# A two-layer encoder trunk whose instructions are recorded first and issued in the order of a list schedule of its own

## The chip, the cores and the metric

One Trainium2 core runs the whole program; the other cores of the chip are idle. The metric is the device time of one execution in microseconds. Times of runs are medians over several executions; durations of single instructions come from one profiled execution. The engines are named as the profile names them: PE is the matmul engine and PEld its weight loads, DVE the vector engine, ACT the scalar engine, POOL the general engine, SP the engine that issues the DMAs. Each engine takes its instructions strictly in the order in which they stand in its own queue, and the queues wait for one another by semaphores.

## The reference

The input is x of 256 tokens by 1024 features in float32. Two layers follow, and a last RMSNorm. A layer, cut to what matters:

```python
h = rmsnorm(x, norm_g[l])
proj = h @ w_in[l]                                   # 1024 x 18688
y_a = hgrn2_mixer(...) * silu(a_g)                   # A: gated recurrence, 8 heads, two directions
y_b = retention_mixer(...) * silu(b_g)               # B: retention, 8 heads, two directions
y_c = rwkv7_mixer(...) * silu(c_g)                   # C: delta rule, 16 heads, two directions
gates = sigmoid(merge.reshape(b, t, 3, D_MODEL))
mixed = gates[0] * (y_a @ w_branch_a) + gates[1] * (y_b @ w_branch_b) + gates[2] * (y_c @ w_branch_c)
x = x + mixed @ w_out
```

## The kernel before, in words

**Weights.** A layer has 93 blocks of weights, 1024 rows by 256 columns, and each block comes in two halves of 128x1024 values (`load_w`, lines 177 to 192). A half is loaded by SP into `wr`; ACT rounds it to float32r into `wh` (line 184); DVE subtracts, `wl = wr - wh` (line 187). Each of the three has a ring of three buffers (`RW = (3, 3, 3)`). A product with h or with a mixer's output is three float32r matmuls per 128 rows (`feat_mm`, line 200, and `tok_mm`, line 210): high by high, high by low, low by high. So a half block feeds 24 matmuls of 256 columns, and the two layers have 2 x 93 x 48 = 8928 of them. All others are float32; in the trace such a matmul stands as two, a transpose as one.

**Mixers.** C works on pairs of heads, p = 0 to 7. `c_prep` (projections `p_rk` and `p_vg`, decays, the products `c_p` of lines 393 to 395 from operands that DVE writes, among them `bbd`, line 388), `c_solve` (the inverse of 32 x 32 blocks: a trip through DRAM into `c_M`, then a chain of small DVE steps that begins at line 425 and goes through `c_tq`, lines 439 to 444) and `c_scan` (the products `c_o`, `c_ox`, `c_oy`, and the state from chunk to chunk, `c_st`, whose copy `c_sb` ACT makes). C runs two pairs ahead (`LA = 2`). Between the pairs stand the parts of A (p = -1 to 2) and of B (p = 3 to 6). A head of A makes its scores in eight steps on one PSUM bank: matmuls into `a_p` (lines 622, 623, 638, 658), then a copy or masked copy by ACT or DVE into `a_pt` (lines 640, 642, 659), then the next step on the same bank. PSUM's eight banks are split as pj 2, c 2, n 2, s 1, ab 1 (`PB`).

**Tail.** `tail` makes the three gates (`p_mg`), the branch products (`t_o`) and `w_out` (`pj`), 28 blocks of a layer; then `norm_T` makes the next layer's h.

**What sets the order.** The code calls the engines directly, in the order of the program text. Tiles come from pools, and the framework's scheduler (`schedule_with_timeline_sim=True`) puts each engine's instructions into their final order when the program is built. A pool that closes between the mixers and the tail gives its memory to the tail's tiles.

Of the kernel before, what the change touches and what calls it, by code (L numbers as in the profile page):

```python
# [2 lines left out]

# [12 lines left out]
L = 2  # L16
D = 1024
# [10 lines left out]
RW = (3, 3, 3)  # L28
# [4 lines left out]
# columns of a layer's packed parameters  # L33
# [9 lines left out]
# columns of the shape constants  # L43
# [9 lines left out]
# of the masks that A takes, and of the rotation that B takes  # L53
# [4 lines left out]
# blocks of weights in a layer, in the order of _blocks()  # L58
# [3 lines left out]
def _blocks():  # L62
    """(key, matrix, row range start, list of (column start, width)) of each block of 1024 rows and 256 columns."""
# [29 lines left out]

@with_exitstack
def trunk(ctx: ExitStack, tc, x, wb, pp, lora, cst, gtab, ng, out, parts="ABCT", layers=L, dbg=None):
    nc = tc.nc
    V, S, G, PE = nc.vector, nc.scalar, nc.gpsimd, nc.tensor

    keep = ctx.enter_context(tc.tile_pool(name="keep", bufs=1))
    wp = ctx.enter_context(tc.tile_pool(name="wp", bufs=1))  # L100
    ps = ctx.enter_context(tc.tile_pool(name="ps", bufs=1, space=bass.MemoryType.PSUM))
    dr = ctx.enter_context(tc.tile_pool(name="dr", bufs=2, space=bass.MemoryType.DRAM))

    S.preload_act_table_set("natural_log_exp_and_others")
# [4 lines left out]
    first = ExitStack()  # L109
    npool = first.enter_context(tc.tile_pool(name="np", bufs=1, side="right"))  # L110
    xs = npool.tile([128, 2, D], F32, name="xs")
    gb = npool.tile([128, D], F32, name="n_g")
    nc.sync.dma_start(xs[:, 0], x_src[:, 0])
    nc.sync.dma_start(C[:, 0:NFST], cst[:, 0:NFST])
    nc.sync.dma_start(xs[:, 1], x_src[:, 1])
    nc.sync.dma_start(gb, ng[0:1].to_broadcast([128, D]))
# [8 lines left out]
    nc.sync.dma_start(C[:, NFST:], cst[:, NFST:NCST])  # L125
    P_ = []
    for l in range(L):
        t = keep.tile([128, NP], F32, name=f"pp{l}")
        nc.sync.dma_start(t, pp[l])
        P_.append(t)  # L130

    turn = {}

    def ring(pool, shape, dt, tag, n, name):
        """a tile in the next of a tag's n buffers, in turn"""
        i = turn[tag] = (turn.get(tag, -1) + 1) % n
        return pool.tile(shape, dt, tag=f"{tag}{i}", bufs=1, name=name)
# [5 lines left out]
    DP = []  # L143
    for l in range(L):
# [3 lines left out]
        # 1 - mu0 - mu1  # L148
# [7 lines left out]
    # lower bounds: softmax over the layers with its maximum, cumulated, less the first  # L156
# [13 lines left out]
    # cumsum - p[0]  # L170
# [6 lines left out]
    def load_w(l, key):  # L177
        """the parts of a block's halves"""
        W = []
        for h in range(2):  # L180
            raw = ring(wp, [128, 1024], F32, "wr", RW[0], "wr")
            nc.sync.dma_start(raw, wb[2 * (l * NBLK + BK[key]) + h])
            hi = ring(wp, [128, 1024], F32R, "wh", RW[1], "wh")
            S.copy(hi, raw)  # L184
            lo = ring(wp, [128, 1024], F32R, "wl", RW[2], "wl")
            n = WS[h]
            V.tensor_sub(lo[:, 0:n], raw[:, 0:n], hi[:, 0:n].bitcast(F32))  # L187
            if n < 1024:
                G.tensor_sub(lo[:, n:], raw[:, n:], hi[:, n:].bitcast(F32))
# [13 lines left out]
    def tok_mm(o, W, t, h):  # L203
        """o[t, column] = h[:, t-tile]^T W; a half of the block holds four k-tiles"""
# [25 lines left out]
    def silu_from(pool, src, shape, tag, tmp, bufs=1, tb=1):  # L230
        """silu of a projection in PSUM"""
# [8 lines left out]
    def norm_T(xs, ss, gb, pool):  # L240
        """xs and the sums of its squares by token; gb: the gains, on every partition"""
# [63 lines left out]
    def c_prep(l, p, codes, pool):  # L305
        """Everything of pair p up to the chunk products, evacuated and masked."""
# [44 lines left out]
        # its ninth block holds the stacked identity  # L351
# [4 lines left out]
        # bonus: sum of r k_d r_k over both directions  # L356
# [7 lines left out]
        # k~, beta~, alpha~, r~ of each direction, and the products within its chunks  # L364
# [6 lines left out]
        for d in range(2):  # L371
            # a chunk's blocks of 64: A_rk^T, r~, A_ak, A_rb^T, beta' (first alpha~), A_ab^T, k', diag g, alpha~^T
            z = pool.tile([128, 4, 9, 64], F32, tag="c_Z", bufs=ZB, name="c_Z")
# [17 lines left out]
            for c in range(4):  # L391
                o = ps.tile([128, 8, 64], F32, tag="c", bufs=PB["c"], name="c_p1")
# [10 lines left out]
    def c_solve(l, p, st, pool):  # L403
        """Inverses of the diagonal 32 x 32 blocks of I - A_ab, one block and every fourth column a partition."""
        Z = st["Z"]
        s1 = dr.tile([4, 8, 32, 32], F32, tag="s1", name="s1")
        for hb in range(4):
            b = hb % 2
            for d in range(2):
                nc.sync.dma_start(s1[hb, 4 * d:4 * d + 4].rearrange("u j i -> j u i"),  # L410
                                  Z[d][32 * hb:32 * hb + 32, :, 5, 32 * b:32 * b + 32])
# [533 lines left out]
```

## Time and profile before

| | us |
|---|---|
| median of 3 runs (1818.41 to 1823.13) | 1823.03 |
| the profiled execution: span from its first to its last instruction | 1821.9 |
| PE busy in it | 1667.6 |
| PEld busy | 1625.0 |
| DVE busy | 1415.4 |
| ACT busy | 1056.5 |
| POOL busy | 322.0 |

Of the profiled execution the trace has its span alone, 1821.9 us, which lies 1.1 us below the median of the runs, so one can be read for the other. In the trace an instruction stands with its start and its duration; a row's last columns tell how long its engine was idle before it and which instruction's end released it. Matmuls overlap: one lasts about 0.28 us from start to result, while the next can start 0.12 us after it, so a PE that is busy need not be a PE at its best rate. PEclk is the granted clock as a share of full speed.

### The profile page before, as it was taken

To read this page: it belongs to the slowest core of one execution; us is meant where nothing else is said; L and a number is where in the kernel's file an instruction comes from. 1 tells how busy PE (TensorE), PEld (TensorE's weight loads), DVE (VectorE), ACT (ScalarE), POOL (GpSimd) and SP (SyncE) were. 2 spreads that over 40 slices of the span, in tenths; PEclk is the share of its full clock that TensorE was granted. 3 is DMA by queue.
4 is the path that set the end of the run, shared out by engine and by line. 5 is a ranking of instruction groups with operands and counts; after the bars stand their busy time and mean duration, and the time that the engine had idled before them with its cause. 6 is when DMAs were issued, how large, how long until landed. Compare 5 with 4: busy or idle time off the path is not lost.

```text
span 1821.9 us, 33791 instructions
## 1 busy us (share of the span) xinstructions
PE 1667.6 (92%) x12960; PEld 1625.0 (89%) x12960; DVE 1415.4 (78%) x2597; ACT 1056.5 (58%) x1940; POOL 322.0 (18%) x312
## 2 busy tenths in 40 slices
PE   6888899999999999999888789988999999999997
PEld 6877899898999998999888788988889999999997
DVE  5799898998878785565657989989998787846554
ACT  5665566757465545555556556757573656456453
POOL 1122222212120200010011222223131202100100
PEclk9989999999999999999988889999999999999999
DMA  6333223324344443755533233233244444437653
GB/s 221 116 118 105 79 96 102 117 86 138 119 155 141 146 148 133 244 200 187 198 114 118 99 100 91 88 109 107 93 133 125 144 142 154 142 131 245 208 186 116
DMA packets 127873, 250.30 MB, mean 137 GB/s; under 512 B 62304, under 2 KB 66784, under 8 KB 127456
## 3 DMA queue, kind: packets, MB, share of 16 engines
q1 hardware_dynamic: 127712, 248.15, 41.6%
q8 instruction: 102, 1.67, 0.4%
q14 instruction: 59, 0.48, 0.1%
HBM read 229.22 MB, written 14.68 MB: 134 GB/s over the span
## 4 chain that ended last, share of the span: by engine, by line
PE 49%; DVE 30%; issue 7%; DMA 6%; ACT 4%; SPq 2%; POOL 0%; DVEq 0%; ACTq 0%; POOLq 0%
PE t_o L200 10%; PE p_mg L200 8%; DVE wl L187 7%; DVE c_tq L439 3%; PE p_bv L210 3%; PE p_vg L200 3%; PE p_bg L200 2%; DMA c_M<-s 2%; PE pj L210 2%; PE c_p L393 2%; DMA s<-c_Z 2%; ACT wh L184 2%; DVE c_ts L441 2%; PE p_rk L200 1%; PE c_p L395 1%
## 5 line engine op out<-in xcount | busy, mean ns | idle before, releaser
L187 DVE TENSOR_TENSOR wl<-wr,wh 128x1024 fp32r<-128x1024 f32 x372 | 475.9, 1280 | 192.3 <-ACT wh L184 190.9
L184 ACT CAST wh<-wr 128x1024 fp32r<-128x1024 f32 x372 | 388.4, 1045 | 272.7 <-PE t_o L200 56.2
L200 PE MATMUL t_o<-yh,wh 128*128 128x256 f32 x512 | 144.7, 284 | 2.8 <-ACT yh L748 2.8
L200 PE MATMUL t_o<-yl,wh 128*128 128x256 f32 x512 | 145.0, 284 | 0.5 <-DVE yl L749 0.5
L200 PE MATMUL t_o<-yh,wl 128*128 128x256 f32 x512 | 144.6, 283 | 0.0
L608 POOL TENSOR_TENSOR a_sl<-a_kq,a_e 128x256 f32<-128x256 f32 x80 | 80.9, 1015 | 230.9 <-ACT a_e L618 66.0
L200 PE MATMUL p_mg<-h_hi,wh 128*128 128x256 f32 x384 | 109.6, 285 | 0.0
L200 PE MATMUL p_mg<-h_hi,wl 128*128 128x256 f32 x384 | 109.4, 285 | 0.0
L200 PE MATMUL p_mg<-h_lo,wh 128*128 128x256 f32 x384 | 108.7, 283 | 0.0
L200 PEld LDWEIGHTS t_o<-yh,wh 128*128 128x128 f32 x512 | 97.6, 191 | 3.2 <-ACT yh L748 3.2
L200 PEld LDWEIGHTS t_o<-yl,wh 128*128 128x128 f32 x512 | 97.9, 191 | 1.0 <-DVE yl L749 0.9
L200 PEld LDWEIGHTS t_o<-yh,wl 128*128 128x128 f32 x512 | 97.9, 191 | 0.0
L393 PE MATMUL c_p<-c_Z,bbd 128*128 128x192 f32 x256 | 68.9, 357 | 29.7 <-DVE bbd L388 25.0
L439 DVE TENSOR_TENSOR c_tq<-W,c_M 128x16 f32<-128x16 f32 (+6 forms) x112 | 89.0, 795 | 1.4
L200 PE MATMUL p_vg<-h_hi,wh 128*128 128x256 f32 x256 | 78.1, 305 | 8.1 <-ACT c_k L288 4.1
L399 ACT COPY c_Z<-c_p 128x192 f32<-128x192 f32 x128 | 40.3, 318 | 74.9 <-DVE c_Z L396 73.7
L200 PE MATMUL p_bg<-h_hi,wl 128*128 128x256 f32 x256 | 75.0, 293 | 4.6 <-DVE wl L187 4.6
L210 PE MATMUL p_bv<-wh,h_hi 128*128 128x256 f32 x256 | 76.1, 297 | 1.1 <-ACT b_z L694 1.1
L210 PE MATMUL p_bv<-wl,h_hi 128*128 128x256 f32 x256 | 75.4, 295 | 1.7 <-DVE wl L187 1.7
L200 PE MATMUL p_vg<-h_lo,wh 128*128 128x256 f32 x256 | 75.8, 296 | 0.0
L200 PE MATMUL p_vg<-h_hi,wl 128*128 128x256 f32 x256 | 75.6, 295 | 0.0
L210 PE MATMUL p_bv<-wh,h_lo 128*128 128x256 f32 x256 | 74.7, 292 | 0.0
(334 smaller groups left out, 5983.3 us busy)
## 6 DMA issues: line engine op xcount, KB each, us to landing
wr<-in_wb_dram SPq DMA_DIRECT2D x372, 512.0 KB, 3.3
c_M<-s SPq DMA_DIRECT2D x64, 128.0 KB, 2.7
c_lt<-in_lora_dram SPq DMA_DIRECT2D x16, 256.0 KB, 2.7
b_sw<-b_z SPq DMA_DIRECT2D x16, 256.0 KB, 3.9
b_gt<-in_gtab_dram SPq DMA_DIRECT2D x16, 256.0 KB, 3.4
yb<-b_y SPq DMA_DIRECT2D x16, 256.0 KB, 3.0
yr<-yb SPq DMA_DIRECT2D x8, 512.0 KB, 5.0
s<-c_Z SPq DMA_DIRECT2D x128, 16.0 KB, 1.9
```

Of the source, the lines that this page charges most:

```text
L184: S.copy(hi, raw)
L187: V.tensor_sub(lo[:, 0:n], raw[:, 0:n], hi[:, 0:n].bitcast(F32))
L200: PE.matmul(o, a[:, k], b[:, k, :], start=(first and n == 0), stop=(last and n == 3 * KT - 1))
L210: PE.matmul(o, a[:, k, t * 128:(t + 1) * 128], b, start=(n == 0), stop=(n == 3 * KT - 1))
L393: PE.matmul(o[:, 2:5], bbd[:, c], z[:, c, 1:8:3], start=True, stop=True)
L395: PE.matmul(o[:, 0:6:5], kbd[:, c], z[:, c, 1:8:6], start=True, stop=True)
L399: S.copy(z[:, c, 4:9:2], o[:, 4:7])
L439: V.tensor_mul(tp, W[:, 0:n, None, 0:j].to_broadcast([128, n, 4, j]), M[:, 0:j, j:j + 4].rearrange("p j i -> p i j")[:, None].to_broadcast ...
L441: V.tensor_reduce(sm, tp, axis=AX.X, op=ALU.add)
L608: G.tensor_mul(s5[:, :, :, 0], k5[:, 0:2, :, 0], e5[:, :, :, 0])
```

## The change

The code of the mixers and of the tail stays as it was, word for word but for the names of engines and pools. What it calls is no longer the engine but a recorder (`Plan`): each call is noted with its engine, its operands, what it must wait for (worked out from the regions of memory that it reads and writes, in pieces of 16 columns by 32 partitions, and from the PSUM bank), and a duration out of a formula per engine and operation (`cost`). When all is noted, `order` runs a list schedule over five engines: at each step the engine that can start first takes, among its ready instructions, the one of lowest rank, `60 * n - depth`, where n is the place in the program and depth the longest chain of durations to the end. It also counts one DMA stream, a lock between DVE and POOL for instructions with two inputs in SBUF, and half clock for PE after a window of little use. `issue` then emits the instructions in that order under the framework's manual schedule.

Tiles have fixed homes: `HOMES` lists regions of SBUF with their widths, and `PLACE` says which names live in which region, at a fixed offset for as long as a mixer or a tail lasts. The weights' rings become three buffers of raw halves and four each of high and of low parts (`RW`). The DMA scratch area is set to 1024.

Both programs hold the same instructions: 11056 matmuls, 2597 of DVE, 1921 of ACT and 822 DMAs stand in the one as in the other, and the same number of banks.

```diff
-PB = {"pj": 2, "c": 2, "n": 2, "s": 1, "ab": 1}
-RW = (3, 3, 3)
+RW = {"in": 3, "hi": 4, "lo": 4}
+HOMES = (("cst", NCST), ("par", 2 * NP + 2 * 74 + 2 * 32 + 2 * 16), ("h_hi", 2048), ("h_lo", 2048),
...
+         ("ab_ex", 2048), ("ab_kq", 1536), ("ab_c", 640), ("ab_e", 2048), ("ab_vg", 1536), ("ab_p", 1344))
+BANKS = (("pj", 2), ("c", 2), ("n", 2), ("s", 1), ("ab", 1))
...
+    def cost(self, eng, op, out, ins, args, kw):
...
+        if eng == "sync":
+            b = size(out) * 4 * out.shape[0]
+            run = min((a.ap[-1][1] if a.ap[-1][0] == 1 else 1) for a in (out, ins[0])) * 4
+            return 380., b / (330. if run >= 512 else 330. * max(run, 64) / 512), both
+        if eng == "tensor":
...
+            elif ins[0].dtype == F32R:
+                g = n / 2.4 + 13
...
+            return g, 163. + g, both
...
+    def order(self):
...
+        rank = self.rank(depth)
...
+        for _ in range(N):
+            at, e = min((now[e] if can[e] else max(now[e], soon[e][0][0]), i)
+                        for i, e in enumerate(ENGINES) if can[e] or soon[e])
...
+            n = heapq.heappop(can[e])[1]
+            o = ops[n]
+            if o[7]:
+                x = "gpsimd" if e == "vector" else "vector"
+                at = max(at, lock[x])
+                lock[e] = at + o[5]
...
+        return sorted(range(N), key=lambda n: (start[n], n))
+
+    def rank(self, depth):
+        return [60. * n - d for n, d in enumerate(depth)]
+
+    def issue(self):
+        self.made = {}
+        with self.tc.manual_schedule():
+            for n in self.order():
+                eng, op, args, kw = self.ops[n][:4]
+                getattr(getattr(self.tc.nc, eng), op)(*map(self.real, args), **{k: self.real(v) for k, v in kw.items()})
...
-            raw = ring(wp, [128, 1024], F32, "wr", RW[0], "wr")
-            nc.sync.dma_start(raw, wb[2 * (l * NBLK + BK[key]) + h])
-            hi = ring(wp, [128, 1024], F32R, "wh", RW[1], "wh")
+            raw, hi, lo = plan.weight()
+            SY.dma_start(raw, wb[2 * (l * NBLK + BK[key]) + h])
             S.copy(hi, raw)
...
-    nc = _bacc.Bacc("TRN2", target_bir_lowering=False, num_devices=1)
+    nc = _bacc.Bacc("TRN2", target_bir_lowering=False, num_devices=1, dynamic_dma_scratch_size=1024)
```

Three places show how the order moves. In the changed program all instructions are issued from one line, and tiles stand under the names of their homes: `c_W` and `c_M` as before, `c_tq` for the steps of `c_solve`, `c_bd` for `bbd` and its like, `c_ux` for `c_uu` and `c_xw`, `c_rkvg` for `c_r` and `c_k`, `ab_` for what A and B use, `pj_` and the like for PSUM banks with their numbers, `w_hi` and `w_lo` for the parts of the weights.

The first place is DVE in layer 0, where the second pair's `c_prep` writes `bbd` while `c_solve` of the first pair runs. Before:

```order
L444 TENSOR_REDUCE W<-c_tq 128x4
L367 TENSOR_TENSOR c_uu<-c_uu,c_k 128x256 x2
L609 TENSOR_TENSOR a_sl<-a_kq,a_e 128x2x8x16
L187 TENSOR_TENSOR wl<-wr,wh 128x1024
L439 TENSOR_TENSOR c_tq<-W,c_M 128x64
L368 TENSOR_TENSOR c_uu<-c_uu,c_ep 128x512
L646 TENSOR_TENSOR a_e<-a_bb 128x512
L388 SCALAR_TENSOR_TENSOR bbd<-c_nkk,c_xw 64x4x64 x2
```

Now:

```order
L451 TENSOR_TENSOR c_ux<-c_ux,c_tu 128x512
L451 TENSOR_REDUCE c_W<-c_tq 128x6x4
L451 TENSOR_TENSOR c_Z_1050<-c_tu,c_ux 128x4x64
L451 TENSOR_TENSOR c_tq<-c_W,c_M 128x784
L451 TENSOR_TENSOR c_Z_1050<-c_rkvg,c_ux 128x4x64
L451 TENSOR_REDUCE c_tq<-c_tq 128x28
L451 SCALAR_TENSOR_TENSOR c_bd<-c_tu,c_ux 64x4x64
L451 TENSOR_TENSOR c_tq<-c_tq,c_M 128x28x4
L451 SCALAR_TENSOR_TENSOR c_bd<-c_tu,c_ux 64x4x64
```

The split of a weight half stood between the steps that lead to `bbd`; now the steps of `c_prep` and of `c_solve` alternate, and the first of the two writes of `bbd` comes six rows after the product with `c_ep` (the first row) with no weight between.

The second place is PE at the same point, where the products `c_p` begin. Before:

```order
L200 MATMUL p_rk<-h_hi,wh 128x256
L200 MATMUL p_rk<-h_lo,wh 128x256
L200 MATMUL p_rk<-h_hi,wl 128x256
L638 MATMUL a_p<-a_sl 128x128 x2
L393 MATMUL c_p_768<-c_Z,bbd 128x192
L394 MATMUL c_p_768<-c_uu,abd 128x2x64
L395 MATMUL c_p_768<-c_Z,kbd 128x2x64
L393 MATMUL c_p_774<-c_Z,bbd 128x192
```

Now:

```order
L451 MATMUL ab_71<-ab_e 128x128 x6
L451 MATMUL pj_65<-h_hi,w_hi_165 128x256
L451 MATMUL pj_65<-h_lo,w_hi_165 128x256
L451 MATMUL ab_71<-ab_kq,ab_p 128x128 x2
L451 MATMUL ab_71<-ab_p,ab_vg 128x256 x2
L451 MATMUL ab_71<-ab_p,cst 128x256
L451 MATMUL c_66<-c_Z_1050,c_bd 128x192
L451 MATMUL c_67<-c_Z_1050,c_bd 128x192
L451 MATMUL c_66<-c_ux,c_bd 128x2x64
```

The last steps of a head of A, which take turns on one bank, now stand next to one another with two matmuls of a weight between them, and right ahead of `c_p`.

The third place is DVE at the first step of a later `c_solve`, which reads what a DMA brings into `c_M`. Before:

```order
L222 TENSOR_SCALAR c_xw<-c_xw 128x2x512
L444 TENSOR_REDUCE W<-c_tq 128x7x4
L187 TENSOR_TENSOR wl<-wr,wh 128x1024 x2
L343 SCALAR_TENSOR_TENSOR c_ep<-cst,c_xw 128x512
L425 TENSOR_TENSOR c_tp<-c_M 128x8x2
L564 TENSOR_SCALAR a_ex<-a_ex 128x1024
```

Now:

```order
L451 SCALAR_TENSOR_TENSOR c_rkvg<-pj_65,par,c_rkvg 128x255
L451 SCALAR_TENSOR_TENSOR c_tu<-c_rkvg,par 128x256
L451 SCALAR_TENSOR_TENSOR c_rkvg<-pj_65,par,c_rkvg 128x255
L451 TENSOR_TENSOR c_y<-n_68,c_Z_584 128x512
L451 TENSOR_TENSOR c_tq<-c_M 128x8x2
L451 TENSOR_SCALAR c_tu<-c_tu 128x256
L451 TENSOR_TENSOR c_M<-c_M,c_tq 128x8
```

Ahead of the step that waits for the DMA stand now the shifts of a pair's r and k and a piece of `c_scan`, where two splits of weights and a scan stood.

More of the change, by code (lines that the diff above doesn't have):

```diff
@@ L91 @@
 assert len(BK) == NBLK
+HOMES = (("cst", NCST), ("par", 2 * NP + 2 * 74 + 2 * 32 + 2 * 16), ("h_hi", 2048), ("h_lo", 2048),
+         ("c_Z0", 2304), ("c_Z1", 2304), ("c_Z2", 2304), ("c_Z3", 2304), ("c_bd", 2048), ("c_wa", 2048),
+         ("c_qm", 2560), ("c_rkvg", 3072), ("c_tu", 2304), ("c_M", 1024), ("c_ux", 2048), ("c_y", 3328), ("c_W", 256), ("c_tq", 812),
+         ("ab_ex", 2048), ("ab_kq", 1536), ("ab_c", 640), ("ab_e", 2048), ("ab_vg", 1536), ("ab_p", 1344))
+PLACE = {
+    "abd": "c_bd", "bbd": "c_bd", "kbd": "c_bd", "vtbd": "c_bd", "w32": "c_wa", "a21": "c_wa", "qp": "c_qm", "mk0": "c_qm", "mk1": "c_qm",
+    "W": "c_W", "c_cw": "c_rkvg", "c_ca": "c_rkvg", "c_r": "c_rkvg", "c_k": "c_rkvg", "c_v": "c_rkvg", "c_g": "c_rkvg",
+    "c_tmp": "c_tu", "c_nkk": "c_tu", "c_bon": "c_tu", "c_ep": "c_tu", "c_lt": "c_ux", "c_uu": "c_ux", "c_xw": "c_ux",
+    "c_M": "c_M", "c_tq": "c_tq", "c_ts": "c_tq", "c_y": "c_y", "c_vb": "c_y", "c_sb": "c_y", "c_os": "c_y",
+    "s_0": "ab_ex", "s_1": "ab_ex", "a_kq": "ab_kq", "ab_c": "ab_c", "s_e": "ab_e", "a_sl": "ab_e", "s_v": "ab_vg", "s_g": "ab_vg",
+    "s_tmp": "ab_vg", "s_p": "ab_p", "a_bb": "ab_p", "a_ks": "ab_p", "a_ng": "ab_p", "b_mv": "ab_p", "b_rs": "ab_p", "b_bs": "ab_p",
+    "yh0": "ab_ex", "yl0": "ab_e", "t_g": "ab_vg", "yr": "ab_p", "t_acc0": "ab_kq", "t_acc1": "ab_kq", "t_acc2": "ab_kq", "t_acc3": "ab_c",
+    "yh1": "c_Z0", "yl1": "c_Z1", "yh2": "c_Z2", "yl2": "c_Z3", "yh3": "c_rkvg", "yl3": "c_tu", "m_hi": "c_wa", "m_lo": "c_qm", "t_xs": "c_bd",
+    "t_gb": "c_M", "t_s4": "c_W", "t_ss": "c_W", "n_rs": "c_W", "n_xn": "c_ux", "t_sq": "c_y", "n_sq": "c_y",
+}
@@ L94, in trunk @@
 @with_exitstack
-def trunk(ctx: ExitStack, tc, x, wb, pp, lora, cst, gtab, ng, out, parts="ABCT", layers=L, dbg=None):
+def trunk(ctx: ExitStack, tc, x, wb, pp, lora, cst, gtab, ng, out):
     nc = tc.nc
[L97 to L104, printed above, removed]
+    nc.scalar.preload_act_table_set("natural_log_exp_and_others")
+    plan = Plan(ctx, tc, x)
+    V, S, G, PE, SY = (plan.engine(n) for n in ("vector", "scalar", "gpsimd", "tensor", "sync"))
+    keep, ps, dr = plan.pool("K"), plan.banks(), plan.dram()
@@ L107, in trunk @@
     x_src = x.rearrange("(t p) d -> p t d", p=128)
     C = keep.tile([128, NCST], F32, name="cst")
[L109 to L116, printed above, removed]
+    npool = plan.pool("T-")
@@ L118, in cc @@
+    xs = npool.tile([128, 2, D], F32, name="t_xs")
+    gb = npool.tile([128, D], F32, name="t_gb")
+    SY.dma_start(xs[:, 0], x_src[:, 0])
+    SY.dma_start(C[:, 0:NFST], cst[:, 0:NFST])
+    SY.dma_start(xs[:, 1], x_src[:, 1])
+    SY.dma_start(gb, ng[0:1].to_broadcast([128, D]))
     def cc(n):
@@ L124, in trunk @@
     EPS = {v: C[:, eo + i:eo + i + 1] for i, v in enumerate((1e-6, 1e-12, 1e-5, 64e-5))}
-    nc.sync.dma_start(C[:, NFST:], cst[:, NFST:NCST])
+    SY.dma_start(C[:, NFST:], cst[:, NFST:NCST])
     P_ = []
@@ L371, in c_prep @@
         for d in range(2):
-            z = pool.tile([128, 4, 9, 64], F32, tag="c_Z", bufs=ZB, name="c_Z")
+            z = pool.tile([128, 4, 9, 64], F32, tag=f"c_Z{(2 * p + d) % ZB}", name="c_Z")
             Z.append(z)
@@ L514, in c_scan @@
             mt.append(m)
-        oc = [ps.tile([128, 4, 64], F32, tag="s", bufs=PB["s"], name="c_oc") for d in range(2)]
+        oc = ps.tile([128, 2, 4, 64], F32, tag="s")
+        oc = [oc[:, d] for d in range(2)]
         sb = [None, None]
@@ L634, in a_head @@
             sl = pairs(e, s)
-            o = ps.tile([128, 2, 128], F32, tag="ab", bufs=PB["ab"], name="a_p")
+            o = ps.tile([128, 2, 128], F32, tag="ab", name="a_p")
             for t in range(2):
@@ L659, in a_head @@
             V.copy_predicated(diag, mask(m), o)
[L661 removed]
+        o = ps.tile([128, 2, T], F32, tag="ab", name="a_o")
         p4 = pt.rearrange("p (j i) k -> p j (i k)", j=2)
@@ L714, in b_pair @@
             V.tensor_mul(pm, o, gt)
-            o = ps.tile([128, 2, T], F32, tag="ab", bufs=PB["ab"], name="b_o")
+            o = ps.tile([128, 2, T], F32, tag="ab", name="b_o")
             for t in range(2):
@@ L763, in tail @@
                     Y += [load_y(src, early, pool if m else early, n) for src, n in (((ya, 0),), ((yb[:, 0:8], 1), (yb[:, 8:16], 2)), ((yc, 3),))[m]]
-                o = [ps.tile([128, 256], F32, tag="c", bufs=PB["c"], name="t_o") for f in range(2)]
+                o = [ps.tile([128, 256], F32, tag="c", name="t_o") for f in range(2)]
                 for i, (key, y) in enumerate(br):
@@ new lines, in final_norm @@
+            SY.dma_start(out[128 * t:128 * t + 128], y[:, t])
+    for l in range(L):
+        pool = abp = plan.pool(f"M{l}")
+        ya, yb, yc = (dr.tile([128, w, T], F32, name="y" + n) for n, w in (("a", 8), ("b", 16), ("c", 8)))
+        c_setup(pool)
+        codes = c_codes(l, pool)
+        st = {}
+        for p in range(-LA, 8):
+            if p >= 0:
+                c_scan(l, p, st.pop(p), pool, yc)
+            if p + LA < 8:
+                st[p + LA] = c_prep(l, p + LA, codes, pool)
+                c_solve(l, p + LA, st[p + LA], pool)
+            for n, i in FILL.get(p, ()):
+                if n == "A":
+                    if i == 0:
+                        for_a(abp)
+                    a_pair(l, i, abp, ya)
+                else:
+                    if i == 0:
+                        for_b(abp)
+                    b_pair(l, i, abp, yb)
+        early = pool = plan.pool(f"T{l}")
+        xs, ss, gb = tail(l, ya, yb, yc, x_src, early, pool)
+        if l + 1 < L:
+            norm_T(xs, ss, gb, pool)
+            x_src = dr.tile([128, 2, D], F32, name="xd")
+            SY.dma_start(x_src, xs)
+        else:
+            final_norm(xs, ss, gb, pool)
@@ L847, in _consts @@
+    plan.issue()
 def _consts():
```

387 lines of the change are left out of this document (302 added, 85 removed).

## The prediction

> **What bounds the kernel now.** I read the page's totals first, then the same columns by stage, then who waits for whom, then the time line at the longest waits.
>
> ```profile
> span 1821.9 us, 33791 instructions
> PE 1667.6 (92%) x12960; PEld 1625.0 (89%) x12960; DVE 1415.4 (78%) x2597; ACT 1056.5 (58%) x1940; POOL 322.0 (18%) x312
> ```
>
> PE is the busiest engine, but its busy time is no measure of its rate, since matmuls overlap. So I take its rate from stretches in which nothing holds it. The next rows are pieces of the chain of waits: start, length, and what ran.
>
> ```profile
> 804.03 11.52 PE t_o L200 x96
> 228.53 0.89 PE c_o L500 x8
> 497.81 1.73 PE b_o L718 x8
> ```
>
> A float32r matmul of 256 columns takes 11.52 / 96 = 0.120 us, a float32 one of 128 columns 0.111, one of 256 columns 0.216. Of the last there are 544 in ten groups; the largest and the smallest group (count, then busy time, mean, idle before) are:
>
> ```profile
> L718 PE MATMUL b_o<-b_v,b_pm 128*128 128x256 f32 x128 | 30.5, 379 | 0.0
> L667 PE MATMUL a_o<-a_rs,cst 128*128 128x256 f32 x32 | 9.5, 378 | 0.0
> ```
>
> The least that PE needs is then 8928 x 0.120 + 544 x 0.216 + 3488 x 0.111 = 1071 + 118 + 387 = 1576 us. The program spends 1821.9, so 246 us are lost in it. Where, the stages tell: start of layer 0, A with C, B with C, tail, then the same for layer 1, then the end. The columns are length, busy time (count) of PE, PEld, DVE, ACT, POOL, then clock, DMA share, GB/s.
>
> ```profile
> 0.00:54.00 54.00, 40.03 (x291) 38.00 (x292) 32.27 (x64) 32.93 (x58) 7.35 (x16) 1.00 0.57 204
> 54.00:436.00 382.00, 338.93 (x2573) 328.13 (x2572) 341.63 (x697) 239.58 (x486) 93.60 (x93) 0.95 0.33 103
> 436.00:741.00 305.00, 290.99 (x2281) 283.22 (x2280) 233.78 (x429) 169.13 (x315) 47.30 (x40) 0.99 0.45 143
> 741.00:899.00 158.00, 156.74 (x1304) 156.28 (x1303) 94.38 (x100) 84.98 (x106) 12.66 (x10) 1.00 0.61 209
> 899.00:956.00 57.00, 47.03 (x337) 44.77 (x336) 32.32 (x49) 30.42 (x60) 7.96 (x13) 0.88 0.41 143
> 956.00:1343.00 387.00, 342.73 (x2568) 332.40 (x2568) 348.43 (x728) 243.43 (x486) 96.91 (x93) 0.93 0.31 100
> 1343.00:1651.00 308.00, 290.09 (x2282) 281.74 (x2281) 234.36 (x429) 170.27 (x318) 43.54 (x40) 0.99 0.45 143
> 1651.00:1807.00 156.00, 154.74 (x1288) 154.28 (x1287) 92.97 (x98) 83.09 (x105) 12.66 (x10) 1.00 0.59 202
> 1807.00:1822.00 15.00, 6.35 (x53) 6.15 (x52) 5.28 (x8) 2.65 (x13) 0.00 (x0) 0.78 0.17 70
> ```
>
> The tails run at PE's rate: 1304 x 0.120 = 156.5 of 158. The loss sits in the mixers. In A with C of layer 0 the projections (lines 200 and 210) are these:
>
> ```profile
> 54.00:436.00 382.00, 174.26 (x1230) 157.85 (x1228) 0.95 0.33 103
> 54.00:436.00 382.00, 34.62 (x215) 30.27 (x216) 0.95 0.33 103
> ```
>
> So 1445 x 0.120 = 173, the other 1128 x 0.111 = 125, and about 130 of these are wide, which adds 130 x 0.105 = 14: PE needs 312 us of 382, 70 are lost. DVE is busy for 341.6 of them, so by DVE only 40 are free. Two engines are nearly full there, and neither reaches its limit, because each waits for the other. The waits that tell most (who, for whom: total, times, longest):
>
> ```profile
> DVE wl L187 <- ACT wh L184: 190.9, 157, 5.3
> PE c_p L393 <- DVE bbd L388: 25.0, 10, 6.6
> DVE c_tp L425 <- DMA c_M<-s: 19.3, 11, 4.8
> ```
>
> The first is harmless in the tails, where DVE has time. The others cost PE. First the one of 6.6 us, on PE, DVE and POOL:
>
> ```profile
> 106.21 0.68 PE L638 MATMUL a_p<-a_sl 128*128 128x128 f32 x4 [0.89 <-POOL c_Z L383]
> 113.49 0.98 PE L393 MATMUL c_p<-c_Z,bbd 128*128 128x192 f32 x2 [6.60 <-DVE bbd L388]
> ```
>
> ```profile
> 107.85 1.75 DVE L187 TENSOR_TENSOR wl<-wr,wh 128x1024 fp32r<-128x1024 f32 x1
> 109.52 1.32 DVE L439 TENSOR_TENSOR c_tq<-W,c_M 128x64 f32<-128x64 f32 x1
> 110.76 1.21 DVE L368 TENSOR_TENSOR c_uu<-c_uu,c_ep 128x512 f32<-128x512 f32 x1
> 111.90 0.68 DVE L646 TENSOR_TENSOR a_e<-a_bb 128x512 f32<-128x512 f32 x1
> 112.50 0.84 DVE L388 SCALAR_TENSOR_TENSOR bbd<-c_nkk,c_xw 64x256 f32<-64x256 f32 x2
> ```
>
> ```profile
> 108.48 2.24 POOL L369 TENSOR_TENSOR c_xw<-c_xw,c_ep 128x512 f32<-128x512 f32 x1
> ```
>
> PE had nothing between `a_p` and `c_p` in its queue while DVE did a weight, a step of the solve and a piece of A ahead of `bbd`, and while POOL worked on `c_xw`, which `bbd` reads: the order of before took `bbd` for earlier than it was. Second, a DVE wait for a DMA that holds up a weight and then PE:
>
> ```profile
> 219.35 0.19 DVE L425 TENSOR_TENSOR c_tp<-c_M 128x16 f32<-128x16 f32 x1 [4.84 <-DMA c_M<-s]
> 219.45 1.79 DVE L187 TENSOR_TENSOR wl<-wr,wh 128x1024 fp32r<-128x1024 f32 x1
> 222.91 1.19 PE L638 MATMUL a_p<-a_sl 128*128 128x128 f32 x4 [4.17 <-DVE a_pt L642]
> ```
>
> **The change part by part.** It removes and adds no instruction, so PE's 1576 us stay; only order and buffers can save. I go by stage and ask what of the loss an order with truer durations can recover.
>
> *A with C, 382 and 387 us.* PE's loss is 70, and in layer 1 387 - 312 = 75. DVE leaves 382 - 341.6 = 40 and 387 - 348.4 = 39. The time that can go lies between nothing and 70 (75). The three places of the order answer to the waits shown: `bbd` no longer stands behind a weight, and ahead of the solve's first step stand short pieces. The longest waits of this kind, 6.6 and 4.8 us, and their like, 25.0 and 19.3 in total, are what a wrong guess costs. I take nearly DVE's room, 36 and 35, because DVE's busy time can itself shrink a little: a weight's split has these durations (minimum, median, maximum):
>
> ```profile
> L187 DVE TENSOR_TENSOR wl<-wr,wh x372: 1160/1225/3411, 15.2 to 1807.2; 128x1024 fp32r<-128x1024 f32 x186
> ```
>
> The two above lasted 1.75 and 1.79, so part of the 342 us is stretch. The Trainium skill, page "SBUF — State Buffer", section "Who interferes with whom", says that a DVE instruction with two SBUF inputs and a POOL instruction that reads SBUF block each other for a whole instruction; the rows at 107.85 and 108.48 agree. By its rule the stretch stays, since the same POOL instructions run. The Trainium skill, page "Perfetto Trace Analysis", section "Identifying the Most-Contended Engine", takes a vector engine's busy share as a fair measure of how near it is to its limit; by it 40 and 39 are the most that can go here, and the sum below keeps within that.
>
> *B with C, 305 and 308 us.* Projections 60 x 24 = 1440 x 0.120 = 173, others 841 x 0.111 = 93, wide ones about 144 x 0.105 = 15: PE needs 281 and loses 24 and 27. DVE is at 77%, so it doesn't bind. Half of it is what I take, 12 and 13, near the idle time that shows, 305 - 291.0 = 14 and 308 - 290.1 = 18; the rest lies within overlapping matmuls or at half clock, which the trace doesn't split for an order.
>
> *Starts.* 291 x 0.120 = 35 of 54, and 337 x 0.120 = 40 of 57: 19 and 17 lost, mostly the load of x, the norm and first projections, a chain that no order shortens. I take 3 and 5, out of nothing to 19 and 17.
>
> *Tails and end.* 1.5, 1.4 and 15 - 6 = 9 us: nothing. The fourth slot of high and low parts matters where DVE is short, in the mixers; in the tails PE is already at its rate. If the fixed homes made the tail wait for the mixers' last reader, it would show at 741; I price that at nothing, since the next blocks' gates need only h and a PSUM bank; without that cover it would be one trip through a DMA and a split, some 5 us (the 4.84 above) per layer.
>
> Sum: 36 + 35 + 12 + 13 + 3 + 5 = 104. 1821.9 - 104 = 1717.9, and with the 1.1 us by which the median of the runs (1823.03) lies above the span, 1719. The bounds of the terms: nothing, 1823; all of PE's rooms, 70 + 75 + 24 + 27 + 19 + 17 + 3 + 9 = 244, 1579. The forecast's own range goes from one and a half times the sum, 1823 - 156 = 1667, to half of it, 1823 - 52 = 1771.
>
> **The rivals.**
>
> *DVE stays as full as it is.* If the two stages of A keep DVE at 342 and 348 us and the waits only move, they give 5 each instead of 71. For it: DVE's share of 89 and 90% there, and the stretch by POOL. Against it: the waits shown end on PE and on DVE in turn, so both had slack. Time: 1823 - (104 - 71 + 10) = 1780.
>
> *Slower: steps without cover.* Counted through the whole order, on the banks ab, c, n and s, a step with less than 0.7 us of other matmuls ahead of it (at the rates above) stood at 121 places before and at 511 now, 41 of them on ab where there was one. The second place of the order shows such a run: the last steps of a head of A with two matmuls between. A step on one bank lasts
>
> ```profile
> L638 PE MATMUL a_p<-a_sl x256: 270/275/553, 103.3 to 1365.2; 128*128 128x128 f32 x128
> L642 DVE COPY_PREDICATED a_pt<-a_c,a_p x48: 423/436/452, 114.0 to 1365.7; 128x256 f32<-128x256 uint32 x48
> ```
>
> 0.275 + 0.436 = 0.71 us and PE stands still for what is not covered. The plan may count on that, where DVE is the bound; but each such step also passes any delay of DVE or ACT to PE at once. With 390 more of them, 104 / 390 = 0.27 us of delay a step undoes the gain; above that the kernel is slower. The stretch of a split seen above, 1.75 - 1.225 = 0.53 us, if it met three in four of these steps, would cost 390 x 0.75 x 0.53 = 155 us: 1719 + 155 = 1874. Against it: n has two banks, so a step there need not wait for the one before, and where DVE binds, PE's standing still is free.
>
> *Nothing changes.* The framework's scheduler orders by durations too. If its misses were replaced by as many others, 1823.
>
> *More than forecast.* If the new order reaches two thirds of PE's room, 163 us: 1660.
>
> **How the numbers follow.** Forecast 0.60, DVE as full as now 0.14, more than forecast 0.07, nothing 0.06, slower 0.13. The predicted time is the forecast's, 1719. Below 1650 lies little of the 0.07, above 1820 lies the slower case and half of the unchanged one, 0.16 together: the range is 1650 to 1820. Faster by over 0.3% (5.5 us, about what a measurement of this kernel can tell from no change) takes in the forecast, DVE as now and more: 0.81; within it 0.06; slower 0.13.
>
> **What would show it.** In the changed kernel PE's busy time should fall by less than the span, and the two stages of A shrink to about 346 and 352 us with DVE over 90% busy in them; the wait of PE for `bbd` (now `c_bd`) should be well under 25 us, that of DVE for `c_M` under 19; the tails should keep 156 to 158 us and full clock. I am wrong by the DVE rival if those stages still take 375 or more at the same DVE time, and by the slower one if PE's waits for steps on ab, n and s add up to over 100 us.

## The result, and the profile after

The changed kernel takes 1758.8 us (median of 4 runs, 1756.9 to 1763.5), the kernel before in the same session 1820.7 us; the ratio is 0.9669, with a 95% interval from 0.9649 to 0.9689. So 62 us are gone where 104 were forecast.

The totals of the changed kernel's page, to be read against the same two lines of before:

```profile
span 1757.2 us, 33751 instructions
PE 1651.2 (94%) x12960; PEld 1607.1 (91%) x12960; DVE 1389.1 (79%) x2597; ACT 1061.7 (60%) x1940; POOL 336.1 (19%) x312
```

The counts of each engine are the same as before. PE's busy time fell by 16 us and the span by 65: most of what went is idle time of PE.

By stage, with the cuts laid at the same weights in both programs (where ACT begins the half block that follows the 12th, 72nd, 132nd and 186th of a layer; for before this moves the cuts of the prediction by at most 4 us), in us:

| kernel | start 0 | A 0 | B 0 | tail 0 | start 1 | A 1 | B 1 | tail 1 | end |
|---|---|---|---|---|---|---|---|---|---|
| before | 52 | 382 | 306 | 158 | 55 | 386 | 311 | 156 | 16 |
| after | 52 | 360 | 295 | 166 | 47 | 361 | 296 | 161 | 19 |

The rows of these stages for the changed kernel (length, busy time and count of PE, PEld, DVE, ACT, POOL, then clock, DMA share, GB/s); first A and B of layer 0, then its tail, then A of layer 1:

```profile
52.00:412.00 360.00, 330.56 (x2533) 317.84 (x2531) 336.13 (x692) 239.74 (x474) 89.94 (x96) 0.95 0.35 108
412.00:707.00 295.00, 288.31 (x2266) 281.68 (x2265) 230.58 (x426) 173.98 (x322) 47.44 (x38) 0.99 0.51 155
707.00:873.00 166.00, 165.75 (x1389) 165.07 (x1388) 92.50 (x111) 86.47 (x115) 18.57 (x10) 1.00 0.58 188
920.00:1281.00 361.00, 327.57 (x2510) 314.66 (x2509) 337.48 (x712) 239.22 (x472) 97.50 (x95) 0.95 0.36 108
```

In A of layer 0 DVE is busy for 336 us where it was 342; its free time went from 40 us to 24, PE's from 43 to 29. The tail grew because it took work over: 1389 matmuls instead of 1304, which at 0.12 us are 10 us, against 8 us more time.

Who waits for whom (total, times, longest):

```profile
PE ab L451 <- DVE ab_e L451: 20.9, 14, 2.8
PE c L451 <- DVE c_bd L451: 10.7, 6, 3.9
PE ab L451 <- DVE ab_p L451: 10.2, 11, 1.8
DVE c_tq L451 <- DMA c_M<-s: 6.0, 2, 3.4
DVE w_lo L451 <- ACT w_hi L451: 163.3, 118, 4.4
```

PE's wait for `bbd` fell from 25.0 to 10.7 us, DVE's wait for the DMA into `c_M` from 19.3 in 11 waits to 6.0 in two. PE's waits for the bank ab, where the steps of A's heads run, grew instead: the two rows on ab above make 31 us, and all rows on this bank add up to 42 us where they made 30 before. The two largest of before are these (`issue`: the profile shows nothing that PE waited for):

```profile
PE a_p L638 <- DVE a_pt L642: 11.2, 7, 4.2
PE a_p L638 <- issue: 7.4, 5, 4.5
```

All of PE's waits together went from 145 to 96 us. The piece of the time line that the orders show, around the first products of the second pair, on PE:

```profile
98.46 0.68 PE L451 MATMUL ab<-ab_e 128*128 128x128 f32 x4 [1.83 <-DVE ab_p L451]
101.48 0.84 PE L451 MATMUL ab<-ab_e 128*128 128x128 f32 x4 [2.34 <-DVE ab_e L451]
103.92 1.22 PE L451 MATMUL ab<-ab_e 128*128 128x128 f32 x4 [1.60 <-DVE ab_p L451]
108.26 2.08 PE L451 MATMUL ab<-ab_p,ab_vg 128*128 128x256 f32 x4 [0.87 <-DVE ab_p L451]
110.85 1.22 PE L451 MATMUL ab<-ab_p,cst 128*128 128x256 f32 x2 [0.52 <-ACT ab_p L451]
115.97 1.62 PE L451 MATMUL c<-c_Z,c_bd 128*128 128x192 f32 x4 [3.89 <-DVE c_bd L451]
```

and on DVE just before the last of them:

```profile
111.76 0.41 DVE L451 TENSOR_TENSOR c_Z<-c_tu,c_ux 128x256 f32<-128x256 f32 x1
112.09 1.48 DVE L451 TENSOR_TENSOR c_tq<-c_W,c_M 128x784 f32<-128x784 f32 x1
113.49 0.42 DVE L451 TENSOR_TENSOR c_Z<-c_rkvg,c_ux 128x256 f32<-128x256 f32 x1
113.83 0.96 DVE L451 TENSOR_REDUCE c_tq<-c_tq 128x28 f32<-128x784 f32 x1
114.71 0.40 DVE L451 SCALAR_TENSOR_TENSOR c_bd<-c_tu,c_ux 64x256 f32<-64x256 f32 x1
115.04 0.33 DVE L451 TENSOR_TENSOR c_tq<-c_tq,c_M 128x112 f32<-128x112 f32 x1
115.40 0.42 DVE L451 SCALAR_TENSOR_TENSOR c_bd<-c_tu,c_ux 64x256 f32<-64x256 f32 x1
```

DVE runs here without a gap and splits no weight, and PE, which has only two matmuls of weights among these steps, stands for 11 us of these 19 in the waits shown. Here the plan lets PE wait: the wait for `bbd` is shorter than the 6.6 us of before, and the steps ahead of it, which matmuls of weights used to cover, now wait too.

### The profile page after: what moved, and what is told of

The parts are those of the page before. It is cut to its first block, busy times and chain, and to the rows that moved or that the text cites. A ratio compares the mean times of both kernels' runs of the same rounds, so it can differ in the third digit from the quotient of the medians.

```text
span 1757.2 us, 33751 instructions
## 1 busy us (share of the span) xinstructions
PE 1651.2 (94%) x12960; PEld 1607.1 (91%) x12960; DVE 1389.1 (79%) x2597; ACT 1061.7 (60%) x1940; POOL 336.1 (19%) x312
## 4 chain that ended last, share of the span: by engine, by line
PE 73%; DVE 15%; ACT 5%; DMA 3%; issue 2%; POOL 0%; SPq 0%; DVEq 0%; POOLq 0%; ACTq 0%
PE pj L451 40%; PE c L451 16%; PE n L451 10%; PE ab L451 6%; DVE ab_e L451 3%; DVE c_tq L451 3%; DVE w_lo L451 2%; PE s L451 2%; ACT w_hi L451 2%; DVE ab_p L451 2%; DVE c_tu L451 1%; ACT ab_e L451 1%; DVE ab_vg L451 1%; DVE c_ux L451 1%; DVE ab_ex L451 1%
## 5 line engine op out<-in xcount | busy, mean ns | idle before, releaser
L451 DVE TENSOR_TENSOR w_lo<-w_in,w_hi 128x1024 fp32r<-128x1024 f32 x372 | 462.8, 1247 | 179.3 <-ACT w_hi L451 163.3
L451 PE MATMUL pj<-h_hi,w_hi 128*128 128x256 f32 x1952 | 560.9, 295 | 5.6 <-ACT ab_ex L451 2.8
L451 PE MATMUL pj<-h_hi,w_lo 128*128 128x256 f32 x1952 | 555.6, 292 | 1.5 <-DVE w_lo L451 1.5
L451 PE MATMUL pj<-h_lo,w_hi 128*128 128x256 f32 x1952 | 556.4, 292 | 0.1
L451 ACT CAST w_hi<-w_in 128x1024 fp32r<-128x1024 f32 x372 | 388.7, 1047 | 269.9 <-PE pj L451 175.7
L451 PEld LDWEIGHTS pj<-h_hi,w_hi 128*128 128x128 f32 x1952 | 368.7, 192 | 9.8 <-ACT ab_ex L451 3.2
L451 PEld LDWEIGHTS pj<-h_hi,w_lo 128*128 128x128 f32 x1952 | 368.7, 192 | 3.7 <-DVE w_lo L451 2.3
L451 PEld LDWEIGHTS pj<-h_lo,w_hi 128*128 128x128 f32 x1952 | 368.5, 192 | 1.9 <-DVE h_lo L451 0.6
L451 PE MATMUL c<-c_Z,c_bd 128*128 128x192 f32 (+1 forms) x512 | 112.3, 322 | 12.2 <-DVE c_bd L451 10.7
L451 PE MATMUL pj<-w_lo,h_hi 128*128 128x256 f32 x384 | 114.2, 297 | 1.3 <-DVE w_lo L451 1.3
L451 PE MATMUL ab<-ab_e 128*128 128x128 f32 x448 | 78.7, 300 | 37.2 <-DVE ab_e L451 20.9
L451 PE MATMUL pj<-w_hi,h_lo 128*128 128x256 f32 x384 | 112.6, 293 | 0.0
```

The lines of the kernel that those rows point to most:

```text
L451: getattr(getattr(self.tc.nc, eng), op)(*map(self.real, args), **{k: self.real(v) for k, v in kw.items()})
```

## The experiments

My theory was that the gain comes from the order, made with truer durations, and that the A stages are then held by DVE. The first rival: the gain comes from the buffers (four slots, fixed homes). The second: what holds the A stages is the row of steps of A's heads on one PSUM bank, whatever the load. All kernels were timed against the kernel before. The rows from "half of DVE's splits" to "all three" leave out part of the computation; they only test what holds the time.

| kernel | median us | ratio to before, interval | A 0, A 1 | B 0, B 1 |
|---|---|---|---|---|
| the change | 1758.8 | 0.9669 [0.9649, 0.9689] | 360, 361 | 295, 296 |
| three slots | 1761.3 | 0.9665 [0.9638, 0.9692] | 364, 377 | 292, 288 |
| framework's order | 1815.2 | 0.996 [0.9941, 0.9978] | 380, 382 | 311, 307 |
| rank without depth | 1798.8 | 0.9868 [0.9837, 0.9899] | 393, 398 | 287, 287 |
| plan without half clock | 1761.8 | 0.9674 [0.9646, 0.9703] | 360, 373 | 293, 291 |
| plan without lock | 1806.5 | 0.9917 [0.9892, 0.9942] | 372, 377 | 304, 305 |
| 300 ns from engine to engine | 1764.9 | 0.97 [0.9671, 0.9729] | 369, 371 | 291, 292 |
| half of DVE's splits | 1747.7 | 0.9599 [0.9564, 0.9634] | 361, 360 | 294, 292 |
| two products instead of three | 1753.0 | 0.962 [0.959, 0.965] | 364, 368 | 294, 293 |
| both of these | 1703.7 | 0.9354 [0.9332, 0.9377] | 345, 345 | 293, 293 |
| fewer steps of A | 1727.0 | 0.948 [0.9453, 0.9506] | 351, 349 | 293, 293 |
| all three | 1654.4 | 0.9081 [0.9053, 0.9109] | 318, 323 | 296, 293 |
| A and B in turn | 1782.8 | 0.9788 [0.9765, 0.9811] | 336, 341 | 330, 336 |

### Order or buffers

**Three slots.**

```diff
-RW = {"in": 3, "hi": 4, "lo": 4}
+RW = {"in": 3, "hi": 3, "lo": 3}
```

> The changed kernel with three slots for the high and low parts of the weights instead of four, planned anew. My theory (the gain comes from the order): the 62 us stay within 10, so 1758 to 1770 us. The rival (the gain comes from buffers: four slots, and homes without pools that close): most of it goes, 1790 us or more.

1761.3 us, a ratio of 0.9665: no difference from four slots. Stages trade time with one another (A of layer 1 is 15 us longer, both stages of B are shorter), the sum stays.

**The framework's order.**

```diff
-        with self.tc.manual_schedule():
-            for n in self.order():
-                eng, op, args, kw = self.ops[n][:4]
...
+        for n in range(len(self.ops)):
+            eng, op, args, kw = self.ops[n][:4]
```

> The changed kernel's homes and four slots, but its instructions are handed to the framework's own scheduler in the program's order. My theory (order): the gain goes, 1805 to 1835 us. The rival (buffers): it stays, 1750 to 1780 us.

1815.2 us. Homes and slots by themselves are worth 0.4%; the order makes the rest. The first rival falls. Its two A stages, 380 and 382 us, are those of before:

```profile
49.00:430.00 381.00, 338.83 (x2549) 328.00 (x2549) 344.79 (x697) 239.30 (x484) 86.96 (x92) 0.94 0.34 103
949.00:1331.00 382.00, 334.10 (x2547) 322.06 (x2547) 347.02 (x730) 244.76 (x489) 89.02 (x92) 0.95 0.34 102
```

### What in the order

**Rank without depth.**

```diff
-        return [60. * n - d for n, d in enumerate(depth)]
+        return [60. * n for n, d in enumerate(depth)]
```

> The changed kernel with the list schedule's rank cut to the place in the program, without the depth of the chain that follows. If true durations alone make the gain, the time is within 15 us of the changed kernel, 1745 to 1775. If it is the preference for long chains, half of the gain or more goes: 1790 or more.

1798.8 us: 1.3% of the 3.3% are left, so more than half of the gain is the preference for what has a long chain behind it. The A stages are even longer than before, 393 and 398 us, while B falls to 287. Durations alone don't make the gain. (This loss and the one of the plan without the lock, below, can't be added: together they exceed the gain.)

**A plan without half clock.**

```diff
-                if halved(int((at + PHASE) // LONG)):
+                if False:
```

> The changed kernel, planned without the half clock: PE is taken to run at full clock always. If the plan's windows of half clock fall where the chip's don't, nothing is lost and 1750 to 1765 us come out. If they fit the chip, losing them costs 10 us or more: over 1769.

1761.8 us: nothing is lost, though A of layer 1 is 12 us longer here too. What the plan knows of the clock has no effect that shows here.

**A plan without the lock between DVE and POOL.**

```diff
-            if o[7]:
+            if False:
```

> The changed kernel, planned without the lock between DVE and POOL: the plan takes their instructions to run side by side. On the chip they still stretch each other. If the plan's knowledge of that matters, the time grows by 10 to 40 us, to 1769 to 1799. If not, it stays at 1753 to 1765.

1806.5 us, 48 more than the change and beyond what I had expected: without this one rule of the plan three quarters of the gain are gone. The instructions are the same, and DVE's busy time in A of layer 0 is 342 us, as before:

```profile
51.00:423.00 372.00, 331.73 (x2524) 316.13 (x2522) 342.17 (x694) 238.04 (x472) 93.70 (x96) 0.96 0.35 105
```

What is lost is the fit of the order: PE's waits add up to 134 us, against 96 in the change. Two rows of them, to be read against 10.2 and 10.7 above:

```profile
PE ab L451 <- DVE ab_p L451: 25.5, 29, 3.2
PE c L451 <- DVE c_bd L451: 19.4, 13, 4.6
```

Not every row grew: that of ab for `ab_e` is 14.0 us, against 20.9. That the longer waits stand where the plan took a DVE instruction to be done too soon is likely, but no run shows it step by step.

**A plan with 300 ns from engine to engine.**

```diff
-        ops, N, HOP = self.ops, len(self.ops), 92.
+        ops, N, HOP = self.ops, len(self.ops), 300.
```

> The changed kernel, planned with 300 ns for a step from one engine to another instead of 92, so that the plan puts more other work between the steps of a chain. If PE's uncovered steps (ab, n) cost what the forecast lacks, the time falls by 10 to 30 us, to 1729 to 1749. If DVE is the bound, cover gives nothing: 1753 to 1775.

1764.9 us, in the range for "cover gives nothing"; the interval of the ratio, 0.9671 to 0.9729, overlaps that of the change. More distance between the steps doesn't help.

### What holds the A stages

Each kernel of this part is planned anew, so its order differs too. Three slots and the plan without half clock show how far a single stage can move by that alone, 12 to 15 us; smaller differences of one stage carry little by themselves.

**Half of DVE's splits.**

```diff
-            V.tensor_sub(lo, raw, hi.bitcast(F32))
+            fresh = lo.offset not in seen
+            seen.add(lo.offset)
+            m = 1024 if fresh or key not in EARLY else 512
+            V.tensor_sub(lo[:, 0:m], raw[:, 0:m], hi[:, 0:m].bitcast(F32))
```

(`EARLY` names the blocks of the A stages, `seen` the slots that have been written once.)

> The changed kernel with less work for DVE: in the blocks of weights of the two A stages (codes, the first six pairs of C, all of A) DVE makes only the first 512 of a half's 1024 low parts; the others keep what stood in the buffer. That takes 66 x 0.54 = 36 us a layer from DVE, and leaves PE's and ACT's work as it is. If DVE bounds these stages (my theory), they shrink by 25 to 35 us each and the time falls by 50 to 70, to 1690 to 1710 us. If PE's own steps on one PSUM bank bound them, it falls by under 20: over 1738.

1747.7 us, 11 less. Against my theory: the A stages stay at 361 and 360 us; what is gained lies in the two starts (48 and 43 instead of 52 and 47) and in single us elsewhere.

```profile
48.00:409.00 361.00, 333.47 (x2550) 321.61 (x2549) 316.79 (x701) 240.76 (x482) 83.87 (x96) 0.96 0.36 109
912.00:1272.00 360.00, 332.38 (x2549) 319.93 (x2547) 324.96 (x732) 245.54 (x485) 86.58 (x96) 0.96 0.36 110
```

DVE's busy time fell by 19 us in A of layer 0 and by 12 in A of layer 1, less than the 36 expected; PE's rose by 3 and 5. DVE's share in the first fell from 93% (336 of 360) to 88%, and the stage did not move. The Trainium skill, page "Perfetto Trace Analysis", section "Identifying the Most-Contended Engine", reads a vector engine's share as its nearness to its limit; here that share said how full DVE was, not that it was the bound.

**Two products instead of three.**

```diff
+        three = ((whi, hhi), (wlo, hhi)) if skip else ((whi, hhi), (whi, hlo), (wlo, hhi))
...
-            for a, b in ((whi, hhi), (whi, hlo), (wlo, hhi)):
+            for a, b in three:
```

(`tok_mm` likewise; `skip` is set for the blocks of the A stages.)

> The changed kernel with less work for PE: in the same blocks the products of the high parts of the weights with h_lo are left out, 66 x 8 matmuls of 0.12 us a layer, 63 us, 127 in all. If DVE bounds the A stages (my theory), the time falls by 50 or less, to 1708 or more. If PE and its steps bound them, it falls by 100 or more, to under 1660.

1753.0 us, 6 less for 127 us less of PE's work, and the A stages even 4 and 7 us longer; the two starts are 8 us shorter each. PE's load alone isn't the bound either.

```profile
44.00:408.00 364.00, 297.87 (x2072) 276.71 (x2072) 333.06 (x699) 239.56 (x477) 96.81 (x96) 0.89 0.37 109
906.00:1274.00 368.00, 302.92 (x2075) 279.46 (x2074) 343.03 (x729) 244.01 (x481) 92.44 (x96) 0.87 0.36 108
```

DVE is still busy for 333 of 364 us and for 343 of 368, and PE's clock in the first of them fell from 0.95 to 0.89.

**Both.** The two edits together.

> The changed kernel with both reliefs at once: half of DVE's low parts and the products with h_lo left out in the blocks of the A stages (36 us of DVE and 63 us of PE a layer). Each alone took 11 and 6 us. Theory of two full engines (DVE and PE bind in turn, so that one relief uncovers the other): the time falls by 60 us or more, to under 1700. Theory of a chain (the steps of A's heads one after the other, whatever the load): it falls by under 30, to over 1730.

1703.7 us, 4 above the range that the theory of two full engines gave, and far from that of a chain. The reliefs that took 11 and 6 us alone take 55 together: DVE and PE do stand in for one another. Of the 55 us, 31 come from the A stages, 15 and 16, and 18 from the two starts. In the A stages DVE is busy for 24 and 17 us less than in the change, PE for 36 and 34:

```profile
44.00:389.00 345.00, 294.54 (x2072) 272.73 (x2072) 311.91 (x692) 238.91 (x477) 86.61 (x96) 0.91 0.38 115
885.00:1230.00 345.00, 293.37 (x2073) 273.30 (x2072) 320.67 (x724) 241.15 (x481) 85.57 (x96) 0.90 0.38 115
```

PE is 85% busy now; DVE is at 90% in layer 0 and at 93% in layer 1, as full as in the change.

**Fewer steps of A.**

```diff
-        for s in (64, 32, 16, 8):
+        for s in (64, 8):
```

> The changed kernel with two of the eight steps of a head of A left out (those of 32 and 16 positions). That takes about 3.3 us of DVE a head, 27 us a layer, and 16 x 2 trips from DVE over ACT, DVE and POOL, PE and back. Theory of a chain: a trip is about 3 us, so the A stages shrink by 35 to 50 us a layer and the time falls by 70 to 100, to under 1690. Theory of two full engines: DVE's 27 us a layer do what the 36 us of the half splits did, 10 to 15 us in all: over 1740.

1727.0 us, between what the two theories gave. The A stages lose 9 and 12 us, 0.6 to 0.8 us for each of the 16 steps left out of a stage, a quarter or less of the 3 us that I took a step's trip to be (the first three steps on ab in the time line above start 3.0 and 2.4 us apart). So A's steps are no chain that sets the time alone.

```profile
51.00:401.00 350.00, 320.18 (x2465) 310.82 (x2465) 312.99 (x634) 228.57 (x458) 76.51 (x80) 0.96 0.38 114
905.00:1254.00 349.00, 318.76 (x2475) 309.16 (x2474) 315.57 (x657) 232.88 (x465) 82.52 (x80) 0.97 0.37 113
```

Here PE is busy for 10 and 9 us less than in the change, about what the stages lost.

**All three.** The edits of the last two, "both" and the fewer steps, together.

> The changed kernel with all three reliefs at once: half of DVE's low parts and the products with h_lo left out in the blocks of the A stages, and the steps of 32 and 16 positions of A's heads left out. Both reliefs of load alone gave 1704 us and A stages of 345 us (by ACT's casts), the fewer steps alone 1727 us and 351. If A's steps are the third thing that holds these stages, the three add up to more than their parts: A stages of 325 us or less, under 1665. If something else holds them at about 345 (C's pairs), it is 335 to 345 and 1680 to 1704. If the three merely add, 335 and 1670 to 1680.

1654.4 us, A stages of 318 and 323. To "both" the fewer steps add 27 and 22 us a stage, where alone they gave 9 and 12.

```profile
42.00:361.00 319.00, 275.82 (x2020) 261.12 (x2019) 286.00 (x626) 226.60 (x462) 72.14 (x80) 0.94 0.42 125
859.00:1183.00 324.00, 279.33 (x2023) 264.89 (x2022) 292.88 (x663) 233.20 (x468) 70.55 (x80) 0.92 0.41 123
```

I had expected this outcome if A's steps are a third thing that holds the stages. But the fewer steps also take load away, and the rows of these kernels fit together without a third bound. Idle time in the two A stages (layer 0, layer 1), in us:

| kernel | stage | PE idle | DVE idle |
|---|---|---|---|
| the change | 360, 361 | 29, 33 | 24, 24 |
| half of DVE's splits | 361, 360 | 28, 28 | 44, 35 |
| fewer steps of A | 350, 349 | 30, 30 | 37, 33 |
| two products | 364, 368 | 66, 65 | 31, 25 |
| both | 345, 345 | 50, 52 | 33, 24 |
| all three | 319, 324 | 43, 45 | 33, 31 |

Where PE keeps its products (the first three rows), it is idle for 28 to 33 us, and the stage follows PE's busy time. Where they are cut (the last three), DVE is idle for 24 to 33 us, and the stage follows DVE's: from "two products" to "both" DVE's busy time falls by 21 and 22 us and the stage by 19 and 23; from "both" to "all three" it falls by 26 and 28 and the stage by 26 and 21. So the loads of DVE and PE, each with some 30 us of idle time that stays, stand at nearly the same height, and that is enough to account for all six kernels. What keeps those 30 us open is not shown. The succession of A's steps may be part of it; no run takes the succession away and leaves the load.

### A version that might be better

**A and B in turn.**

```diff
-FILL = {-1: ("A0",), 0: ("A1",), 1: ("A2",), 2: ("A3",), 3: ("B0",), 4: ("B1",), 5: ("B2",), 6: ("B3",)}
+FILL = {-1: ("A0",), 0: ("B0",), 1: ("A1",), 2: ("B1",), 3: ("A2",), 4: ("B2",), 5: ("A3",), 6: ("B3",)}
...
-                    if i == 0:
-                        for_a(abp)
+                    for_a(abp)
```

(and the same for `for_b`)

> The changed kernel with A and B alternating (A0, B0, A1, B1 and so on beside the pairs of C) instead of all of A first; the masks and the rotation are loaded anew each time (8 loads of 256 to 320 KB a layer instead of 2). Theory of two full engines: DVE's load spreads over the whole mixer stage and PE's with it, 15 to 40 us less, 1720 to 1745. Theory of a chain: A's heads get twice the time for the same steps, 30 to 60 us less, under 1730. If neither holds, the time stays within 8 of 1759.

1782.8 us, 24 more than the change: both expectations fall. The load does spread. In layer 0 DVE is busy for 292 of 336 us and for 284 of 330 (the two halves of the mixers, at the cuts of A and B above):

```profile
52.00:388.00 336.00, 308.33 (x2346) 297.85 (x2345) 291.82 (x569) 206.42 (x408) 74.12 (x70) 0.95 0.42 125
388.00:718.00 330.00, 314.01 (x2464) 304.92 (x2463) 283.83 (x555) 206.77 (x394) 64.09 (x64) 0.98 0.45 138
```

Yet the two together take 666 us instead of 655. PE loses 28 us in the first and 16 in the second, where the change loses 29 and 7. Spreading gave the first half nothing back in PE's idle time and cost the second 9; why, these runs don't tell. None of the kernels that compute the whole is faster than the change.

## Why the prediction came out as it did, point by point

*The direction and its cause.* The gain comes from the order, as argued: the same instructions and homes in the framework's order give 0.996. The places named are the ones that moved (`bbd` 25.0 to 10.7 us, `c_M` 19.3 to 6.0).

*A with C: the term that was too large.* I took 36 and 35 us, "nearly DVE's room". Measured are 22 and 25, and of these some 5 us each are matmuls that now run elsewhere (2533 instead of 2572 in layer 0 and 2510 instead of 2561 in layer 1, at 0.12 us). The step that failed is to take DVE's idle time in a stage as time that an order can recover. DVE's idle time shrank from 40 to 24 us and PE's from 43 to 29, and the reliefs show that such a stage keeps 24 to 33 us of idle time on whichever of the two holds it; only what lay above that was there for this list schedule to win. The waits that the term rested on, for `bbd` and for `c_M`, also held 44 us in total, less than the 71 taken from them, and they fell by 28. That DVE bounds the stage, which the DVE rival rests on, is refuted as far as a single bound goes: less DVE work alone moved the A stages by nothing. The prediction let the stretch of DVE by POOL stay as it was, beside a guess that DVE's busy time could shrink a little: it shrank by 26 us over the program with the same instructions (1415.4 to 1389.1), 13 of them in the splits of weights (475.9 to 462.8).

*B with C.* 12 and 13 forecast, 11 and 15 measured.

*Starts.* 3 and 5 forecast, 0 and 8 measured; that the sum agrees is luck.

*Tails and end.* Nothing forecast; measured 8, 5 and 3 us longer, the tails because 85 and 60 matmuls more run there, 17 us of work for 13 us of time. PE is busy for 165.75 of the 166 us of the first tail, so the homes cost nothing there. The sign that I gave, tails of 156 to 158 us, did not hold, since the forecast had no term for work that moves between stages.

*The slots.* I priced the fourth slot at no more than a help in the mixers; it is worth nothing that can be measured.

*The rival of steps without cover.* Its mechanism is in the trace: PE's waits on ab rose from 30 to 42 us. But on ab, n and s together they make 52, where over 100 was to be its sign, and with 300 ns a step in the plan, which asks for more cover, nothing is gained. The delay that I feared for every uncovered step, DVE's stretch by POOL, is in the plan, and planning without the lock costs 48 us. That the change escaped this rival because the plan counts the stretch is my reading; no run counts the delays at the uncovered steps. The Trainium skill, page "SBUF — State Buffer", section "Who interferes with whom", describes the block that this rule of the plan models; the runs agree that it matters, 1806.5 against 1758.8 us.

*The sum.* 65 us of span against 104. By stage, 14 and 10 are missing in A, 13 in the tails and 3 in the end; B gave 1 more than forecast and the starts what was forecast. The tails' part is work moved out of the stages before.

## What to carry to other kernels

When two engines are each about 90% busy in a stage and wait for each other, the idle time of either is not what a better order wins: here it won about a third of PE's room, and in that stage taking away half of DVE's splits alone, or a third of PE's products alone, won nothing. A list schedule's value lay in two rules, preferring what has a long chain behind it and counting the stretch between DVE and POOL; a slot more and a model of the clock gave nothing. To find out what holds such a stage, take loads away one at a time and then together: only the pair shows that the bounds stand at the same height. A probe that takes out steps takes out load as well, so read the busy times before you call the steps a bound.

## What the runs showed of the hardware

Less work for PE went with a lower clock: with a third of the projections' matmuls in the A stages left out, the granted clock in A of layer 0 was 0.89 instead of 0.95, and over the whole run 0.946 instead of 0.973. The records of the granted clock in these traces know two values, full and half. So 2 x 0.11 x 364 = 80 us of the stage ran at half clock instead of 2 x 0.05 x 360 = 36, which costs (80 - 36) / 2 = 22 us of PE's time. That fits the busy times: 461 matmuls fewer at 0.12 us are 55 us, and PE's busy time in the stage fell by 33. The Trainium skill, page "TensorE: Matmul & The Clock Gate", Part 1, says that the gate follows how busy PE has been of late; the rows agree, and part of a relief for PE is lost that way when something else holds the stage.

A split of 128x1024 values, on DVE, took 1.225 us by the median and 1.75 and 1.79 us beside POOL's work in the rows before the change. The same list schedule took 1758.8 us when it counted such a block and 1806.5 when it did not.
